# A decoder layer's weights: the low part made by an accumulating transfer instead of a subtraction

## The chip, the cores and the metric

The kernel runs on one core of a Trainium2 chip. The metric is the device time of one execution in microseconds; lower is better. An engine takes its instructions in the order in which the program gives them, and waits on semaphores for what other engines and transfers produce.

## The reference

One layer of a hybrid decoder on 512 tokens of width 1024, all in float32. The input is RMS-normalised and goes through one input projection. Three head groups read it: sparse attention (compressed, selected and window branches, with softmax and gates), a Mamba-2 SSD scan, and cross-attention to 256 memory tokens. Their outputs are gated, concatenated, projected back and added to the input, and normalised again.

```python
def reference(x, mem, positions, g_in, w_in, ...):
    xn = _rmsnorm(h, g_in[l])
    proj = xn @ w_in[l]
    (q_a, k_c, v_c, k_s, v_s, k_w, v_w, gate_logits, gate_a,
     z, xbc, dt, q_x, gate_x) = jnp.split(proj, split_at, axis=-1)
    o_a = _nsa_mixer(q_a, k_c, v_c, ...) * jax.nn.silu(gate_a)
    o_b = _ssd_mixer(z, xbc, dt, ...)
    o_c = _memory_attention(q_x, mem, ...) * jax.nn.silu(gate_x)
    h = h + jnp.concatenate([o_a, o_b, o_c], axis=-1) @ w_out[l]
    return _rmsnorm(h, g_final)
```

## The kernel before

**Two parts of each operand.** Matmuls run on operands of the type float32r, which holds fewer bits than float32. To keep the precision, every operand is split: `hi` is the value rounded to float32r, `lo` is the value minus `hi`. A product is then three matmuls: hi by hi, lo by hi, hi by lo.

**Weights come in chunks.** `chunk` (line 379) loads up to 1024 columns on 128 partitions (512 KB) into a staging tile `wst`, copies it to `whi` on ScalarE or VectorE (`X.copy`), and subtracts to get `wlo` on VectorE or GpSimd (`X.tensor_tensor`). There are 64 chunks. `wst` has two slots (`WS`), `whi` and `wlo` three each (`WH`). A slot is taken by the next chunk when the last reader of the old one is done: for `wst` that is the subtraction, for `whi` and `wlo` a matmul. The loads are issued by SP.

**Who uses them.** `proj_d` (line 450) takes one chunk for 128 output columns: eight steps of three matmuls on 512 columns, in the order hi, lo, hi, so that the lo part is needed in the second matmul. `z_half` takes three chunks at the start (the first half) and two later, and reads their lo parts last. `values` holds three chunks through its loop; `compress_mlp`, `mem_k` and `mem_v` are the short projections of the compressed and memory branches; `out_part` and `out_proj` make the output projection.

**Order.** Instructions are not issued where they are written. `Program` records them with their operands, and `issue` (line 173) places them by a list scheduler: each engine takes, of the instructions whose operands and slots are there, the first of the program (shifted by biases). `cost` (line 137) gives the scheduler a duration for each instruction and a time to land for each transfer; where two engines may run an instruction, the one that is free takes it, VectorE ahead of ScalarE and GpSimd. So a changed instruction or cost changes the whole order. All instructions are issued on one line, so the profile names nearly all of them L278, and tiles tell them apart. The stages, in time: the start and the first half of `z` to about 31 us; the SSD inputs and the second half of `z` to 92; compressed and memory keys and values beside the SSD scan to 182; keys and values of the other branches to 216; attention, woven with cross-attention and the output projection of two groups, to 440; the rest of the output projection.

Of the kernel before, what the change touches and what calls it, by code (L numbers as in the profile page):

```python
# [13 lines left out]
AF = mybir.ActivationFunctionType  # L14
OP = mybir.AluOpType
# [18 lines left out]
WMAX = 1024  # L34
# slots of the tags in SBUF and PSUM
B4, T2, M8, QB, PB, XB_, WS, WH = 2, 5, 12, 5, 4, 2, 2, 3
SB, TB, JB = 2, 2, 3
# shares at which streams are interleaved, and how far their instructions are put before (-) or
# behind (+) their place in the program when more than one could go
SA, SX, WA, WX, R1, R2 = 18.0, 55.0, 60.0, 128.0, 12.0, 5.0  # L40
# [34 lines left out]
class Program:  # L75
    """The instructions of a kernel, recorded in program order and issued in the order of a list
    scheduler: each engine takes, of the instructions whose operands and tiles are there, the
    first of the program. A tile takes a slot of its tag only if the tiles of the program before
    it still find theirs."""

# [31 lines left out]
    def record(self, *ways):  # L112
        """One instruction, with each engine that may run it: (engine, function, args, kw)."""
        eng, fn, args, kw = ways[0]
        outs = [a for a in (kw.get("out", args[0] if args else None), kw.get("accum_out")) if a is not None]
        ins = [a for a in list(args[0 if "out" in kw else 1:]) + [v for k, v in kw.items() if k not in ("out", "accum_out")]
               if hasattr(a, "tensor")]
        op = {"eng": eng, "fn": fn, "n": len(self.ops), "deps": set(), "bias": self.bias + BIAS.get((outs[0].tensor.name.rsplit("_", 1)[0], fn), 0), "tiles": set(),
              "args": args, "kw": kw, "ways": {w[0]: w + self.cost(w[0], w[1], outs, ins, w[3]) for w in ways}}
        op["cost"], op["tail"] = op["ways"][eng][4:]  # L120
        for aps, write in ((ins, False), (outs, True)):
            for a in aps:
                t, p0, p1, m = self.region(a)
                tl = self.tiles.setdefault(t, {"tag": None, "psum": False, "acc": [], "users": 0, "dram": True})
                op["tiles"].add(t)
                for o, w, q0, q1, m2 in tl["acc"]:
                    if (write or w) and o is not op and q0 < p1 and p0 < q1 and m & m2:
                        op["deps"].add(o["n"])
                tl["acc"].append((op, write, p0, p1, m))
        for t in op["tiles"]:  # L130
            tl = self.tiles[t]
            tl["users"] += 1
            if tl["users"] == 1 and tl["tag"] is not None:
                self.tags[tl["tag"]]["q"].append(t)
        self.ops.append(op)

    def cost(self, eng, fn, outs, ins, kw):
        n = 1
        for d in outs[0].shape[1:]:
            n *= d  # L140
        ps = any(self.tiles.get(a.tensor.name, {}).get("psum") for a in outs[:1] + ins)
        if fn == "dma_start":
            b = 4 * n * outs[0].shape[0]
            return 60.0, 2000.0 + b / 360.0
        if eng == "PE":
            if fn == "transpose":
                return 109.5, 158.0
            if ins[0].dtype == F32R:
                return max(109.5, 0.4167 * n + 2.5), 158.0
            return max(214.0 * ins[0].shape[1] / P, 1.667 * n), 158.0  # L150
        scalars = sum(1 for a in ins if hasattr(a, "tensor") and len(a.shape) == 2 and a.shape[1] == 1)
        if eng == "ACT":
            return (51.0 if ps else 93.0) + 0.833 * n + 93.0 * (scalars + ("accum_out" in kw)), 110.0
        if eng == "DVE":
            k = 1.04
            if fn == "reciprocal":
                k = 6.25
            elif fn == "tensor_reduce" or fn == "stream_shuffle":
                n = 1
                for d in ins[0].shape[1:]:  # L160
                    n *= d
            elif fn in ("tensor_copy", "tensor_scalar") and not ps:
                k = 0.52
            return 68.0 + k * n + 62.0 * scalars * (n > 1), 92.0
        if fn == "tensor_scalar" and scalars == 1:
            return 260.0 + 3.33 * n, 30.0
        if fn == "tensor_scalar":
            return 327.0 + 0.833 * n, 30.0
        if kw.get("op") == OP.pow:
            return 464.0, 30.0  # L170
        return 150.0 + 2.1 * n, 30.0
# [118 lines left out]
class AnyEngine:  # L290
    """Instructions that more than one engine can run."""

# [32 lines left out]
def hymba_kernel(ctx: ExitStack, tc: tile.TileContext, A, out):  # L325
# [3 lines left out]
    X = AnyEngine(prog)  # L329
# [7 lines left out]
    def f(ap):  # L337
        return ap.bitcast(F32)
# [8 lines left out]

# [1 line left out]
    def load_x(to, eng, i):  # L349
# [18 lines left out]

# [1 line left out]
    def biased(b, gen):  # L370
# [7 lines left out]

    def chunk(src, n, st=None, first=False):
        if st is None:  # L380
            st = wp.tile([P, WMAX], F32, name="wst", tag="wst", bufs=WS)[:, :n]
        SY.dma_start(st, src)
        hi = wp.tile([P, WMAX], F32R, name="whi", tag="whi", bufs=WH)[:, :n]
        lo = wp.tile([P, WMAX], F32R, name="wlo", tag="wlo", bufs=WH)[:, :n]
        if first:
            SC.activation(hi, st, AF.Copy)
        else:
            X.copy(hi, st)
        X.tensor_tensor(lo, st, f(hi), op=OP.subtract)
        return hi, lo  # L390

# [1 line left out]
    def rstd_of(ss, n, name):  # L393
# [26 lines left out]

# [1 line left out]
    rc = cp.tile([P, S], F32, name="rc")  # L422
# [23 lines left out]

# [1 line left out]
    done = set()  # L448
# [24 lines left out]

    # compressed keys and values: blocks of 32 tokens, every 16
    def compress_in(c0, pcol):
# [81 lines left out]

    # keys of the selected and the window branch
    def keys(b, c0):
# [13 lines left out]

    # values of both branches and the gates: token rows
    def values():
# [43 lines left out]

# [1 line left out]
    def cmp_soft(t):  # L621
# [40 lines left out]
    def soft(t, i, unit, den, ps2):  # L662
        """Scores of a unit of (head, branch) pairs and their exponentials, with the sums."""
        g, n, u = t // 2, i + 1, len(unit)
        s = pp.tile([P, u, n * P], F32, name="sc2", tag="s", bufs=SB)
        for x in range(0, u, 2):
            e, b = unit[x]
# [13 lines left out]
    def soft_div(t, i, units, den, ps):  # L681
        """Exponentials by their sums, times the gates."""
        gate = AT["gate"]
# [16 lines left out]
    def apply(t, i, ps2, pcs):  # L700
# [19 lines left out]
        if i % 2:  # L720
            # both parts together, times the gate path
            pov = O["po"]
# [45 lines left out]

# [1 line left out]
    def mem_turn(m):  # L770
# [101 lines left out]

# [1 line left out]
    SD = {}  # L874
# [87 lines left out]
    def z_half(hf):  # L962
# [6 lines left out]
        for c in range(3 - hf):  # L969
            n = min(kc_, KT - kc_ * c) * w_  # L970
            st = kp.tile([P, WMAX], F32, name="wst0", tag="m8", bufs=M8)[:, :n] if hf == 0 and c == 2 else None
            ch.append(chunk(A[f"wz{hf}"][c][:, :n], n, st, hf == c == 0))
            if hf == 0 and c < 2:
                load_x(xt, SY, 2 + c)
# [99 lines left out]

# [1 line left out]
    acc = []  # L1076

    def out_part(part):
        """The share of head group B or C, onto the residual."""
        if not acc:  # L1080
# [72 lines left out]
    def weave(a, b, ca, cb):  # L1153
        """Both streams, each at its share of the tensor engine's time."""
        pa = pb = 0.0
# [20 lines left out]
    def inter(a, b, ca, cb):  # L1176
        """Both streams as one, each at its share."""
        pa = pb = 0.0
# [63 lines left out]

# d-major columns of the input projection, by tiles of 128
DCOLS = [(c, P) for c in (KC, VC, KS, KW)]
# [5 lines left out]
def layout(inputs):  # L1250
    """The inputs as the program reads them: slices, transposes and packing only."""
    f32 = np.float32
# [3 lines left out]
    def rows(m, k, c):  # L1256
        # [k*128, c] -> [128, k*c]
        return m.reshape(k, P, c).transpose(1, 0, 2).reshape(P, k * c)
# [60 lines left out]
```

## Time and profile before

| | |
|---|---|
| time, median of 3 runs | 473.93 us (473.19 to 474.29) |
| profiled execution, first to last instruction | 473.4 us |
| TensorE / VectorE / ScalarE / GpSimd busy | 418.8 / 405.6 / 180.5 / 209.8 us |
| loaded from and written to HBM | 42.43 MB and 2.11 MB, 94 GB/s over the span |
| share of the 16 DMA engines' time, SP's queue | 28.6% |

The median of the runs is 0.5 us above the profiled span. Busy times of engines overlap. Matmuls are pipelined: a matmul's row is longer than the time until the next one starts.

### The profile page before, as it was taken

Reading aid. Unit: us, or ns where it says so; the run is one execution under the profiler, and the core shown is the slowest. Engines: PE = TensorE matmul, PEld = TensorE weight load, DVE = VectorE, ACT = ScalarE, POOL = GpSimd, SP = SyncE. Lnnn points to the kernel's source line nnn. Section 1 sums busy time; section 2 is a strip of 40 time slices with the busy share of each in tenths; the row PEclk is TensorE's granted clock in tenths of the full one; section 3 lists DMA queues with packets and bytes.
Section 4 is the critical chain, followed back from the end, with each engine's and each line's share of the span. In section 5 each row is a group of like instructions: output and inputs, shape, how many; then the busy total and the mean of one; then the engine's idle time right before and its main releaser. Section 6 shows DMA issues by size and latency. Waiting matters only on the chain.

```text
span 473.4 us, 6323 instructions
## 1 busy us (share of the span) xinstructions
PE 418.8 (88%) x2291; PEld 350.0 (74%) x2291; DVE 405.6 (86%) x701; ACT 180.5 (38%) x402; POOL 209.8 (44%) x137
## 2 busy tenths in 40 slices
PE   3798969898796999998998997989989999799993
PEld 3786869678785888896877775868678776687872
DVE  4897886998999998898789999897998999968555
ACT  5333232544224023444444344434444435322324
POOL 3671322367576675624443224233434626402332
PEclk9898979999999899999999999899999999999998
DMA  8714520333553444213120120132113202203104
GB/s 321 266 53 131 174 66 4 111 112 94 174 160 108 134 134 141 90 45 132 48 90 0 46 79 11 46 134 90 44 46 126 97 0 91 61 29 90 44 1 177
DMA packets 15407, 44.95 MB, mean 95 GB/s; under 512 B 1648, under 2 KB 3984, under 8 KB 15376
## 3 DMA queue, kind: packets, MB, share of 16 engines
q1 hardware_dynamic: 15232, 44.54, 28.6%
q8 instruction: 18, 0.29, 0.3%
q14 instruction: 13, 0.11, 0.1%
q10 hardware_dynamic: 144, 0.01, 0.0%
HBM read 42.43 MB, written 2.11 MB: 94 GB/s over the span
## 4 chain that ended last, share of the span: by engine, by line
PE 42%; DVE 40%; issue 5%; ACT 3%; POOL 2%; DMA 1%; POOLq 0%; DVEq 0%; ACTq 0%
PE pj L278 13%; PE po L278 9%; PE pop L278 5%; DVE wlo L278 5%; DVE whi L278 5%; PE pt L278 3%; DVE den L278 3%; DVE pr L278 3%; PE pjz L278 3%; PE sc L278 2%; PE pjv L278 2%; DVE cacc L278 2%; DVE nm L278 2%; DVE ptl L278 2%; DVE o L278 2%
## 5 line engine op out<-in xcount | busy, mean ns | idle before, releaser
L278 POOL TENSOR_TENSOR wlo<-wst,whi 128x1024 fp32r<-128x1024 f32 (+2 forms) x34 | 82.2, 2419 | 97.7 <-DVE whi L278 33.9
L278 PE MATMUL pj<-xh,whi 128*128 128x512 f32 x224 | 91.4, 408 | 0.0
L278 PE MATMUL pj<-xh,wlo 128*128 128x512 f32 x224 | 90.5, 404 | 0.4 <-DVE wlo L278 0.3
L278 PE MATMUL pj<-xl,whi 128*128 128x512 f32 x224 | 89.9, 401 | 0.0
L278 PEld LDWEIGHTS pj<-xh,wlo 128*128 128x128 f32 x224 | 42.7, 190 | 8.8 <-DVE wlo L278 0.9
L278 PEld LDWEIGHTS pj<-xl,whi 128*128 128x128 f32 x224 | 42.7, 191 | 8.6 <-issue 0.3
L278 PEld LDWEIGHTS pj<-xh,whi 128*128 128x128 f32 x224 | 42.7, 190 | 7.9 <-DVE gxt L278 0.4
L278 DVE TENSOR_TENSOR wlo<-wst,whi 128x1024 fp32r<-128x1024 f32 (+2 forms) x30 | 45.7, 1522 | 1.8 <-PE pjz L278 0.7
L278 ACT ACTIVATE pr<-sc,nm 128x128 f32<-128x128 f32 (+3 forms) x64 | 33.2, 525 | 36.1 <-DVE nm L278 16.5
L278 ACT ACTIVATE whi<-wst 128x1024 fp32r<-128x1024 f32 (+3 forms) x31 | 31.7, 1023 | 25.4 <-DMA wst<-in_wd 5.9
L278 PE MATMUL pt<-cst,pr 128*128 128x128 f32 x160 | 31.4, 279 | 8.7 <-DVE pr L278 6.9
L278 DVE CAST whi<-wst 128x1024 fp32r<-128x1024 f32 (+1 forms) x33 | 32.2, 977 | 6.6 <-PE pj L278 3.4
L278 PEld LDWEIGHTS pt<-cst,pr 128*128 128x128 f32 x160 | 19.4, 140 | 16.4 <-DVE pr L278 9.1
L278 PE MATMUL sc<-kst,qst 128*128 128x512 f32 (+2 forms) x96 | 29.5, 368 | 1.1 <-ACT pr L278 1.1
L278 DVE TENSOR_TENSOR ptl<-pt,pth 128x512 fp32r<-128x512 f32 x40 | 27.1, 682 | 1.4 <-ACT pth L278 1.0
L278 DVE TENSOR_REDUCE nm<-sc 128x1 f32<-128x384 f32 (+3 forms) x44 | 27.7, 633 | 0.3
L278 POOL TENSOR_SCALAR pr<-pr,den,gate 128x512 f32<-128x512 f32 (+1 forms) x11 | 9.0, 821 | 40.6 <-DVE den L278 24.9
L278 PE MATMUL pop<-whi,oph 128*128 128x512 f32 x64 | 26.4, 415 | 0.1
L278 ACT ACTIVATE pth<-pt 128x512 fp32r<-128x512 f32 x23 | 13.7, 596 | 33.2 <-PE pt L278 33.1
L278 PE MATMUL pop<-whi,opl 128*128 128x512 f32 x64 | 25.6, 403 | 0.0
L278 PE MATMUL pop<-wlo,oph 128*128 128x512 f32 x64 | 25.5, 401 | 0.0
L278 PE MATMUL po<-ptl,vst 128*128 128x256 f32 x80 | 22.0, 293 | 1.7 <-DVE ptl L278 1.7
(287 smaller groups left out, 1076.1 us busy)
## 6 DMA issues: line engine op xcount, KB each, us to landing
wst<-in_wd SPq DMA_DIRECT2D x28, 512.0 KB, 3.3
x<-in_x SPq DMA_DIRECT2D x8, 512.0 KB, 4.2
R<-a_rows SPq DMA_DIRECT2D x4, 512.0 KB, 4.3
wst<-in_w1k SPq DMA_DIRECT2D x4, 512.0 KB, 3.5
wst<-in_wmk SPq DMA_DIRECT2D x4, 512.0 KB, 3.6
wst<-in_w1v SPq DMA_DIRECT2D x4, 512.0 KB, 3.5
wst<-in_wmv SPq DMA_DIRECT2D x4, 512.0 KB, 3.6
wst<-in_wob SPq DMA_DIRECT2D x4, 512.0 KB, 3.6
```

Of the source, the lines that this page charges most:

```text
L278: o["ins"] = getattr(self.engines[o["eng"]].engine, o["fn"])(*o["args"], **o["kw"])
```

## The change

For all chunks but the first three (the first half of `z`), the subtraction goes. ScalarE writes the negated, rounded weights into `wlo` (`scale=-1.0`), the hi copy stays as it was, and GpSimd's queue issues a second transfer of the same weights from HBM that adds to what lies in `wlo`. The staging tile is now read by the two copies alone. The scheduler's costs get an entry for a transfer issued by GpSimd.

```diff
@@ cost
         if fn == "dma_start":
             b = 4 * n * outs[0].shape[0]
+            if eng == "POOL":
+                return 1000.0, 2000.0 + b / 180.0
             return 60.0, 2000.0 + b / 360.0
@@ chunk
-    def chunk(src, n, st=None, first=False):
+    def chunk(src, n, st=None, first=None):
...
         SY.dma_start(st, src)
         hi = wp.tile([P, WMAX], F32R, name="whi", tag="whi", bufs=WH)[:, :n]
         lo = wp.tile([P, WMAX], F32R, name="wlo", tag="wlo", bufs=WH)[:, :n]
-        if first:
-            SC.activation(hi, st, AF.Copy)
-        else:
-            X.copy(hi, st)
-        X.tensor_tensor(lo, st, f(hi), op=OP.subtract)
+        if first is not None:
+            if first:
+                SC.activation(hi, st, AF.Copy)
+            else:
+                X.copy(hi, st)
+            X.tensor_tensor(lo, st, f(hi), op=OP.subtract)
+            return hi, lo
+        SC.activation(lo, st, AF.Copy, scale=-1.0)
+        X.copy(hi, st)
+        G.dma_start(lo, src, accum_op=OP.add)
         return hi, lo
@@ z_half
-            ch.append(chunk(A[f"wz{hf}"][c][:, :n], n, st, hf == c == 0))
+            ch.append(chunk(A[f"wz{hf}"][c][:, :n], n, st, c == 0 if hf == 0 else None))
```

The rest of the diff takes out comments.

## Rows read from the trace of the kernel before

**Rows 1.** The page's busy time of each engine: us, share of the span, instructions.

```profile
PE 418.8 (88%) x2291; PEld 350.0 (74%) x2291; DVE 405.6 (86%) x701; ACT 180.5 (38%) x402; POOL 209.8 (44%) x137
```

**Rows 2.** The chain that ended last, whole span: shares by engine, then by line.

```profile
PE 42%; DVE 40%; issue 5%; ACT 3%; POOL 2%; DMA 1%; POOLq 0%; DVEq 0%; ACTq 0%
PE pj L278 13%; PE po L278 9%; PE pop L278 5%; DVE wlo L278 5%; DVE whi L278 5%; PE pt L278 3%; DVE den L278 3%; DVE pr L278 3%; PE pjz L278 3%; PE sc L278 2%; PE pjv L278 2%; DVE cacc L278 2%; DVE nm L278 2%; DVE ptl L278 2%; DVE o L278 2%
```

**Rows 3.** The same chain in two windows, 92 to 182 and 216 to 440 us.

```profile
by line: DVE wlo L278 20.6%; DVE whi L278 14.4%; PE pjm L278 8.0%; issue 7.4%; PE ph L278 5.6%; DVE cacc L278 4.6%; DMA wst<-in_wmk 4.0%; DMA wst<-in_wd 3.7%; DVE bct L278 2.6%; DVE kc L278 2.5%; PE pj L278 2.3%; DVE ft L278 2.3%; DVE vcs L
...
by line: PE pj L278 24.1%; PE pop L278 9.9%; PE po L278 8.0%; PE pt L278 6.3%; DVE den L278 5.7%; DVE pr L278 5.2%; PE sc L278 4.5%; DVE ptl L278 3.5%; DVE nm L278 3.4%; DVE o L278 3.2%; issue 3.2%; DVE xnm L278 2.3%; DVE whi L278 2.3%; DVE
```

**Rows 4.** Windows, all engines: stretch, length, busy (instructions) by engine, PEclk, DMA share, GB/s.

```profile
92.00:182.00 90.00, 76.86 (x502) 68.68 (x501) 83.57 (x106) 28.09 (x51) 59.15 (x36) 0.98 0.41 129
216.00:440.00 224.00, 210.08 (x1092) 167.25 (x1092) 200.18 (x394) 92.72 (x236) 83.58 (x54) 0.99 0.20 64
```

**Rows 5.** Windows for the instructions that touch `wlo`: PE, PEld, VectorE, GpSimd.

```profile
31.00:92.00 61.00, 26.88 (x88) 15.37 (x87) 5.04 (x5) 12.87 (x5) 0.92 0.32 100
92.00:182.00 90.00, 41.64 (x131) 25.45 (x131) 24.39 (x17) 12.34 (x5) 0.98 0.41 129
...
216.00:440.00 224.00, 70.51 (x174) 33.13 (x174) 4.41 (x3) 46.21 (x19) 0.99 0.20 64
```

**Rows 6.** Waits of SP's queue: us in total, times, longest.

```profile
SPq L278 <- POOL wlo L278: 222.9, 31, 15.3
```

**Rows 7.** The page's costliest groups: busy us, mean ns, idle before.

```profile
L278 POOL TENSOR_TENSOR wlo<-wst,whi 128x1024 fp32r<-128x1024 f32 (+2 forms) x34 | 82.2, 2419 | 97.7 <-DVE whi L278 33.9
...
L278 DVE TENSOR_TENSOR wlo<-wst,whi 128x1024 fp32r<-128x1024 f32 (+2 forms) x30 | 45.7, 1522 | 1.8 <-PE pjz L278 0.7
```

**Rows 8.** Instructions on tile `wst`: ns min/median/max, first and last start; landing of its loads.

```profile
L278 DVE CAST whi<-wst x33: 423/694/2506, 14.8 to 448.6; 128x1024 fp32r<-128x1024 f32 x32, 128x528 fp32r<-128x528 f32 x1
L278 ACT ACTIVATE whi<-wst x31: 672/1058/1073, 7.3 to 443.1; 128x1024 fp32r<-128x1024 f32 x26, 128x792 fp32r<-128x792 f32 x2, 128x840 fp32r<-128x840 f32 x2, 128x560 fp32r<-128x560 f32 x1
...
DMA to landing us min/median/max: 2.6/3.5/9.1
```

**Rows 9.** Instructions on tile `den`, 216 to 440 us: ns min/median/max.

```profile
L278 DVE TENSOR_SCALAR den<-den x26: 154/160/2166, 223.0 to 429.3; 128x2 f32<-128x2 f32 x23, 128x4 f32<-128x4 f32 x3
...
L278 DVE TENSOR_SCALAR pr<-pr,den,gate x21: 465/548/2502, 228.0 to 430.7; 128x384 f32<-128x384 f32 x11, 128x512 f32<-128x512 f32 x10
```

**Rows 10.** VectorE's groups by shape, 216 to 440 us: busy us, mean ns.

```profile
L278 DVE TENSOR_SCALAR den<-den 128x2 f32<-128x2 f32 x23 | 11.3, 492 | 0.9 <-ACT pr L278 0.8
L278 DVE CAST whi<-wst 128x1024 fp32r<-128x1024 f32 x10 | 8.7, 867 | 0.3 <-PE pj L278 0.2
L278 DVE TENSOR_SCALAR pr<-pr,den,gate 128x384 f32<-128x384 f32 x11 | 8.1, 761 | 0.1
L278 DVE TENSOR_SCALAR pr<-pr,den,gate 128x512 f32<-128x512 f32 x10 | 7.9, 806 | 0.1
```

**Rows 11.** A one-column instruction among GpSimd's groups, whole span.

```profile
L278 POOL TENSOR_TENSOR rx<-rx,mhalf 128x1 f32<-128x1 f32 x6 | 4.7, 781 | 7.3 <-DVE rx L278 6.5 <-DVE cwh L278 0.8
```

**Rows 12.** Windows, all engines, the first 20 us.

```profile
0.00:20.00 20.00, 10.30 (x51) 9.62 (x52) 12.17 (x25) 9.86 (x17) 11.52 (x13) 0.91 0.94 336
```

**Rows 13.** Timeline, 30 to 32 us: start, length, instruction.

```profile
30.61 1.23 DVE L278 TENSOR_TENSOR wlo<-wst,whi 128x1024 fp32r<-128x1024 f32 x1 [0.66 <-PE pjz L278]
...
31.89 0.50 PE L278 MATMUL pj<-xh,wlo 128*128 128x512 f32 x1 [0.25 <-DVE wlo L278]
```

**Rows 14.** Timeline, 207 to 217 us.

```profile
207.86 1.06 ACT L278 ACTIVATE whi<-wst 128x1024 fp32r<-128x1024 f32 x1 [0.99 <-PE pjv L278]
...
210.31 0.41 PE L278 MATMUL pj<-xh,wlo 128*128 128x512 f32 x1
```

**Rows 15.** Timeline, 448 to 456 us.

```profile
448.63 0.69 DVE L278 CAST whi<-wst 128x1024 fp32r<-128x1024 f32 x1
...
454.96 0.40 PE L278 MATMUL po<-wlo,oh 128*128 128x512 f32 x1
```

## The prediction, made before the changed kernel ran

> **What bounds the kernel now.** I read the busy times first [rows 1]: TensorE 88%, VectorE 86%, ScalarE 38%, GpSimd 44%. Two engines are near full, so the next view is the chain that ended last [rows 2]: 42% of it on TensorE and 40% on VectorE, with the weights' `wlo` and `whi` at 5.0% and 4.7% of 473.4 us, that is 24 and 22 us. What the change removes is therefore partly on the path. Where it is, the chain of two windows tells [rows 3]. From 92 to 182 us (compressed keys and values, memory keys and values, SSD) `wlo` is 20.6% and `whi` 14.4% of the window, 18.5 and 13.0 us, so four fifths of `wlo`'s share of the chain lie here. From 216 to 440 us (attention) `whi` has 2.3%, `wlo` is not among the parts listed, and `den` and `pr`, small VectorE work of the softmax, hold 10.9%.
>
> Then the stages. From 92 to 182 us VectorE is busy 83.6 of 90 us [rows 4], of which 24.4 are `wlo`, and 22 lo parts are made (17 on VectorE, 5 on GpSimd) [rows 5]: 4.1 us a chunk. The waits of SP's queue [rows 6] say how chunks follow one another: a load waits for a `wlo` (222.9 us in 31 waits for GpSimd's alone), because the subtraction is the last reader of the staging slot, and there are two slots.
>
> **What goes.** All subtractions but those of the first three chunks: 61 of 64. VectorE's 30 cost 45.7 us and GpSimd's 34 cost 82.2 [rows 7]; about 44 and 78 of these go. GpSimd's also cost VectorE: a `whi` cast takes 423 to 2506 ns with a median of 694 [rows 8], and the one-pass `den` instruction 154 to 2166 with a median of 160 [rows 9]; the long ones stand beside GpSimd work. In the attention stage I count 23 `den` x (492 - 160) = 7.6 us, 21 `pr` x (782 - 548) = 4.9 and 10 `whi` x (867 - 694) = 1.7 [rows 8 to 10], 14.2 us in all. The subtractions are 46.2 of GpSimd's 83.6 busy us there [rows 4, 5], 55%, so 7.8 us of this is theirs.
>
> **What comes.** Per chunk: a negating ScalarE copy, 1.06 us by the copy of the same shape [rows 8], so 61 x 1.06 = 64 us and ScalarE goes from 180.5 to about 244 us, 52%; it hides in ScalarE's idle time, and in the attention stage with it the exponentials queued behind. The `whi` copy stays; a busier ScalarE may leave more of them to VectorE (0 to 29 x 0.69 = 20 us; I take 4 us, since the negation is done first and VectorE is seldom free). And a transfer issued by GpSimd, in whose queue the softmax scalings and SSD products wait behind it. No GpSimd transfer is in this trace. Its issue I bound by nothing below and above by one of its subtractions, 2.4 us [rows 7]; I take 0.78, the mean of GpSimd's one-column instruction [rows 11], since an issue touches no data. The Trainium skill, "DMA: Bandwidth & Descriptors", section Specifications, gives about 1 us to the first byte on this path; with it each chunk below is 0.2 us later, which no run here shows.
>
> Its landing: a plain 512 KB load takes 3.5 us in the median, 2.6 at least and 9.1 at most [rows 8]. The accumulate also reads its destination. In the first 20 us the engines move 336 GB/s at a share of 0.94 [rows 12], so 512 KB occupy all sixteen for 524288 B / 357 GB/s = 1.47 us; a second read adds 0 to 1.47. I take it whole: 5.0 us. The Trainium skill, "Collectives: The Full Stack", section "The bandwidth ceiling", finds an adding transfer at about half of a copy's rate because of its two source reads; by that the sum is the same, and plain transfers alone, as here, cannot show it.
>
> So from a free `wlo` slot to a ready lo part: 1.06 + 0.78 + 5.0 = 6.8 us (2.6 + 1.06 = 3.7 to 9.1 + 1.06 + 2.4 = 12.6), against 1.2 to 2.4 for the subtraction. TensorE needs lo in the second matmul of a chunk, so this is a stall wherever a slot comes free just ahead of its use.
>
> **The places.**
> Start: the first new-style chunk's slot comes free at 30.61 and its lo part is first used at 31.89 [rows 13]. New: 30.61 + 6.8 = 37.4, +5.5 us (+2.4 to +11.3). Nothing covers it: TensorE has only this chunk.
> 31 to 92 us: VectorE loses 5.0 us of `wlo` [rows 5]; at the chain's 40% share, -2 (0 to -5).
> 92 to 182 us: four limits, each for 22 chunks. VectorE falls to 83.6 - 24.4 = 59 us and is out. Staging: a slot is free after load and copies, (3.5 + 1.06)/2 = 2.3 us a chunk, 50 us. The three `wlo` slots: (6.8 + about 1.5 of waiting in ScalarE's and GpSimd's queues + some 2 of use)/3 = 3.4 us, 76 us; the 1.5 is an estimate from GpSimd's 59 busy us of 90. The DMA engines: now 0.41 of the time [rows 4], 37 us; the accumulates add 22 x 1.47 to 22 x 2.94, so 69 to 102 us. With the second read whole it is 102, less about 10 for chunks whose transfers lie ahead of the window: 92, against 90 now. I take +2 (-21 to +12). So the work that VectorE loses here is replaced by transfers that take about as long.
> Behind the values' projection, whose three chunks hold all three slots: the next slot's copy starts at 207.9, lo is first used at 210.31 [rows 14]. New 214.7, +4.4; the scores and the softmax of attention's first tile are there to be put ahead, so I take +3 (0 to +8).
> Attention: VectorE loses 4.4 us of `wlo` [rows 5] and 7.8 of blocking, gets back 4 of `whi` and, if a transfer's issue blocks as GpSimd's other work does, 19 x 0.78 / 46.2 of the 7.8, 2.5. GpSimd, freed, takes scalings that either engine can run: of VectorE's 16 us of `pr` [rows 10] I take a quarter, 4. Together -9.7; of `den` and `pr`, whose rows make 27 us, the chain holds 24 (10.9% of 224), but a chain that is relieved in one place passes to TensorE, whose `pj` alone has 24.1% of it: I take two thirds, -6 (-16 to 0). The later lo parts are hidden here: a chunk comes every 11 us or so, three slots deep.
> End: the last chunk's copy starts at 448.63; 455.4 against a use at 454.96 [rows 15]: +0.5 (0 to +6).
> Sum: 5.5 - 2 + 2 + 3 - 6 + 0.5 = +3.0 on the profiled span of 473.4; the median of the runs, 473.93, is 0.5 us more, so 476.9, say 477.
>
> **Rivals.** *One: faster.* The accumulate costs the DMA engines what a plain load does (3.5 us to land, 1.47 of occupation). Then the dense window is 69 us, -21; the start +4, behind the values +1.5, the end 0; attention -13, 31 to 92 -4: 473.9 - 32 = 442 at the far end; with half of the window's gain and the -6 in attention it is 473.9 - 11 + 5.5 - 6 - 4 = 458. It decides if the landing is under about 4.5 us. For it: the chain, which has 31.5 us of `whi` and `wlo` in that window; against it: the destination has to be read too.
> *Two: slower by much.* The casts that last up to 2506 ns show that VectorE and GpSimd hold something from one another; if GpSimd's issue has to wait likewise for VectorE, which is busy 93% of the dense window, each lo part is up to 2.5 us later: 22 x 2.5/3 = 18 in the dense window, 2.5 at each of three turns: 477 + 26 = 503. The Trainium skill, "SBUF — State Buffer", section "SBUF: two separate sides", states just this of transfers issued by GpSimd: VectorE's two-port operations keep it from writing descriptors (0.62 us becomes 3.1). Against it: VectorE's casts of this kind are short, 0.69 us.
> *Three: no change.* Relief and delay cancel: 473.9.
> *Four: faster without the transfers' help.* The blocking counts for all of its length in attention, -16 in place of -6: 477 - 10 = 467. For it: `den` and `pr` are on the chain there. Against it: `pj` alone holds 24.1% of that chain.
> *Five: VectorE is not relieved,* since it takes nearly all `whi` copies (20 us back): attention and the early part give nothing, 477 + 8 = 485.
>
> **How the numbers follow.** The measurement tells 0.2%, 0.95 us, from no change. Forecast (slower, 475 to 489, its own range): 0.33. Rival one 0.26; two 0.12; three 0.08; four 0.15; five 0.06. Faster 0.26 + 0.15 = 0.41, same 0.08, slower 0.33 + 0.12 + 0.06 = 0.51. The two signs share the chance, so the range for 8 in 10 reaches into rivals one and two: 450 to 500, leaving out the far gain of rival one and the far end of rival two.
>
> **What would show it.** Of the changed profile: no `wlo` subtraction behind the third; 61 ScalarE `wlo` copies of 1.06 us; POOL's busy time down by some 78 us; `den` and `whi` means nearer their medians; issue to landing near 5 us (under 4.5 speaks for rival one, over 7.5 for two); a TensorE gap near 31 to 37 us on the first transfer; DMA share from 92 to 182 us at 0.9 or more; VectorE below 70% there. I am wrong if TensorE never waits for those transfers, or if the dense window shrinks by over 10 us.

## The result, and the profile of the changed kernel

The changed kernel takes 507.16 us (median of 4 runs, 504.22 to 516.37) against 474.11 (473.19 to 475.93) for the kernel before: a ratio of 1.0664 with a 95% interval of 1.0614 to 1.0715. Forecast were 477 us, with 450 to 500 as the range. The profiled execution is the longest of the four, so its stages lose 41 us where the medians differ by 33; in a run with the same edits up to the values' projection (e5_early below, span 504.5 us instead of 514.6) the stretch up to there is 6 us shorter.

The busy times and the chain that ended last, against [rows 1, 2], and the DMA queues (packets, MB, share of the 16 engines):

```profile
PE 433.7 (84%) x2291; PEld 364.0 (71%) x2291; DVE 352.7 (69%) x701; ACT 219.9 (43%) x436; POOL 167.9 (33%) x164
...
q0 software_dynamic: 8784, 31.56, 34.8%
q1 hardware_dynamic: 15232, 44.54, 26.8%
...
PE 51%; DMA 20%; DVE 12%; issue 8%; POOL 4%; ACT 4%; POOLq 0%; DVEq 0%; SPq 0%
PE pj L280 26%; DMA wlo<-in_wd 7%; PE pop L280 5%; PE po L280 4%; PE pt L280 3%; PE pjz L280 3%; PE sc L280 3%; DMA wlo<-in_wox 3%; DVE whi L280 2%; DMA wst<-in_wmv 2%; DMA R<-a_rows 2%; DMA wlo<-in_wmk 2%; DMA wlo<-in_w1v 2%; DVE o L280 1%; ACT wlo L280 1%
```

VectorE lost 53 us of work, and its share of the chain fell from 40% to 12%. In its place stand transfers, 20% of the chain where they had 1%. The accumulates' queue, q0, takes 34.8% of 514.6 us, 179 us for 61 chunks, 2.94 us each. A plain load of as many bytes takes 1.6: q1's 26.8% for 44.54 MB.

The windows of [rows 4], and the waits of TensorE (us in total, times, longest):

```profile
92.00:182.00 90.00, 67.06 (x359) 58.04 (x359) 58.19 (x83) 31.39 (x47) 41.65 (x39) 0.88 0.83 189
216.00:440.00 224.00, 209.53 (x1102) 171.02 (x1101) 179.65 (x394) 110.09 (x256) 62.24 (x64) 0.98 0.55 126
```

```profile
PE pj L280 <- DMA wlo<-in_wd: 19.0, 4, 9.6
```

In the dense window VectorE falls from 83.6 to 58.2 busy us and TensorE does 359 matmuls where it did 502: a resource was freed and less was done. The DMA engines' share doubles, to 0.83.

One new chunk, the first, in the timeline (start, length), against [rows 13]:

```profile
32.30 1.04 ACT L280 ACTIVATE wlo<-wst 128x1024 fp32r<-128x1024 f32 x1
...
33.66 1.05 POOL L280 DMA_DIRECT2D wlo<-in_wd  x1 [1.97 <-ACT th L280]
...
42.60 0.80 PE L280 MATMUL pj<-xh,wlo 128*128 128x512 f32 x1 [9.64 <-DMA wlo<-in_wd]
```

The negation takes 1.04 us, the issue follows 0.3 us behind it, and the lo part is there 8.9 us after the issue began; TensorE waits 9.64 us. Over all chunks, issue to landing, first of the transfers into `wlo`:

```profile
DMA to landing us min/median/max: 5.2/7.6/11.4
```

and of the loads into `wst`, which took 2.6/3.5/9.1 before [rows 8]:

```profile
DMA to landing us min/median/max: 2.6/5.5/9.8
```

Where the 41 us between the two spans lie, by the first matmul that reads the lo part of a kind of chunk (for `pjv` also the last matmul, for `pop` the first of any part). Times are in us; the runs are those of the next section, and those with four slots have eleven big tiles instead of twelve:

| stretch | before | after | small, 3 slots | 4 slots | 4 slots, plain | subtraction, 4 slots | late, 4 slots |
|---|---|---|---|---|---|---|---|
| start to the first `pj` with lo | 31.9 | 42.6 | 39.0 | 34.0 | 33.0 | 34.8 | 34.7 |
| to the values' projection (`pjv`) | 162.8 | 191.1 | 169.5 | 166.4 | 161.0 | 160.3 | 160.8 |
| the values' projection | 15.5 | 16.0 | 14.5 | 17.9 | 17.5 | 17.5 | 17.5 |
| its end to the first `pop` | 158.2 | 157.9 | 151.3 | 151.2 | 149.2 | 165.8 | 149.1 |
| to the end | 105.0 | 107.0 | 103.0 | 101.5 | 102.5 | 106.2 | 103.9 |
| span | 473.4 | 514.6 | 477.3 | 471.0 | 463.2 | 484.6 | 466.0 |

Of the 41.2 us, 10.7 are the start and 28.3 the stretch up to the values' projection.

### The profile page after: what moved, and what is told of

It reads as the page before. It is cut to its first block, busy times and chain, and to the rows that moved or that the text cites. A ratio compares the mean times of both kernels' runs of the same rounds, so it can differ in the third digit from the quotient of the medians.

```text
span 514.6 us, 6447 instructions
## 1 busy us (share of the span) xinstructions
PE 433.7 (84%) x2291; PEld 364.0 (71%) x2291; DVE 352.7 (69%) x701; ACT 219.9 (43%) x436; POOL 167.9 (33%) x164
## 3 DMA queue, kind: packets, MB, share of 16 engines
q0 software_dynamic: 8784, 31.56, 34.8%
q1 hardware_dynamic: 15232, 44.54, 26.8%
## 4 chain that ended last, share of the span: by engine, by line
PE 51%; DMA 20%; DVE 12%; issue 8%; POOL 4%; ACT 4%; POOLq 0%; DVEq 0%; SPq 0%
PE pj L280 26%; DMA wlo<-in_wd 7%; PE pop L280 5%; PE po L280 4%; PE pt L280 3%; PE pjz L280 3%; PE sc L280 3%; DMA wlo<-in_wox 3%; DVE whi L280 2%; DMA wst<-in_wmv 2%; DMA R<-a_rows 2%; DMA wlo<-in_wmk 2%; DMA wlo<-in_w1v 2%; DVE o L280 1%; ACT wlo L280 1%
## 5 line engine op out<-in xcount | busy, mean ns | idle before, releaser
L280 ACT ACTIVATE wlo<-wst 128x1024 fp32r<-128x1024 f32 (+2 forms) x61 | 63.8, 1046 | 112.5 <-PE pj L280 48.6
L280 PE MATMUL pj<-xh,wlo 128*128 128x512 f32 x224 | 93.4, 417 | 19.0 <-DMA wlo<-in_wd 19.0
L280 PE MATMUL pj<-xh,whi 128*128 128x512 f32 x224 | 93.2, 417 | 3.4 <-DVE whi L280 3.1
L280 PE MATMUL pj<-xl,whi 128*128 128x512 f32 x224 | 91.5, 408 | 0.0
L280 DVE CAST whi<-wst 128x1024 fp32r<-128x1024 f32 (+1 forms) x41 | 36.9, 901 | 34.6 <-PE pj L280 22.7
L280 POOL DMA_DIRECT2D wlo<-in_wd x28 | 25.0, 892 | 104.1 <-ACT wlo L280 94.3
L280 DVE CAST pth<-pt 128x512 fp32r<-128x512 f32 x23 | 15.8, 688 | 20.8 <-PE pt L280 20.6
L280 POOL TENSOR_SCALAR pr<-pr,den,gate 128x512 f32<-128x512 f32 (+1 forms) x14 | 11.3, 807 | 45.8 <-DVE den L280 39.5
L280 PE MATMUL po<-pth,vst 128*128 128x256 f32 x80 | 22.7, 288 | 3.7 <-DVE pth L280 3.7
L280 ACT ACTIVATE whi<-wst 128x1024 fp32r<-128x1024 f32 (+3 forms) x23 | 22.9, 1000 | 3.3 <-PE pjz L280 3.3
```

The costliest lines, as they stand in the source:

```text
L280: o["ins"] = getattr(self.engines[o["eng"]].engine, o["fn"])(*o["args"], **o["kw"])
```

## Experiments

The kernel before was timed again beside these runs, with medians of 474.75 to 475.73 us; ratios are against those.

### What one transfer costs

**e1_probe.** No layer is computed; single transfers of 512 KB run one at a time, and then in company.

```diff
+nc.gpsimd.dma_start(x, A[r], accum_op=OP.add)      # alone, three times
+nc.gpsimd.dma_start(x, A[3], accum_op=OP.add)      # two in flight
+nc.gpsimd.dma_start(y, A[4], accum_op=OP.add)
+nc.gpsimd.dma_start(x, A[5], accum_op=OP.add)      # beside two loads of SP
+nc.sync.dma_start(l1, A[6])
+nc.sync.dma_start(l2, A[7])
```

> This kernel does nothing of the layer: it only loads 512 KB weight tiles, one transfer at a time and then in company. It asks what an accumulating transfer costs by itself. Theory L (latency: the 7.6 us in the changed kernel are what such a transfer takes even alone, and three lo slots cannot cover it): the accumulate takes 6.5 to 8 us alone from issue to landing, the half-sized one over 5.5, and company adds under 1 us. Theory O (occupation: the engines have too many bytes to move): about 5 us alone (3.5 for a load, 1.5 for the second read), half-sized about 4; 7.5 or more beside another accumulate or beside two loads of SP, and those loads go from 3.5 to 5 or more. Theory S (VectorE's casts hold up GpSimd's issue): about 5 us alone and 7.5 or more beside ten casts, with an issue that lengthens from 0.9 us. GpSimd's plain transfer: L 5 us or more, O and S about 4.

The page's DMA issues (count, KB each, median us from issue to landing):

```profile
sp<-in_wd SPq DMA_DIRECT2D x3, 512.0 KB, 3.2
plain<-in_wd POOLq DMA_DIRECT2D x3, 512.0 KB, 3.6
acc<-in_wd POOLq DMA_DIRECT2D x3, 512.0 KB, 5.1
mixl<-in_wd SPq DMA_DIRECT2D x2, 512.0 KB, 4.4
castacc<-in_wd POOLq DMA_DIRECT2D x2, 512.0 KB, 5.5
half<-in_wd POOLq DMA_DIRECT2D x3, 256.0 KB, 3.6
...
pairy<-in_wd POOLq DMA_DIRECT2D x1, 512.0 KB, 5.1
pairx<-in_wd POOLq DMA_DIRECT2D x1, 512.0 KB, 7.1
mixacc<-in_wd POOLq DMA_DIRECT2D x1, 512.0 KB, 8.1
```

Alone an accumulate lands 5.1 us after its issue began, 1.5 later than the plain copy of the same queue. Half the bytes take 1.5 us less. Beside two loads it takes 8.1, and the loads 4.4 instead of 3.2. Beside ten casts of VectorE, issued with it, it takes 5.5. So company on the DMA engines is enough to explain the 7.6 us in the kernel. Ten casts of VectorE, the mechanism of rival two, account for 0.4.

### Which part of the transfer the kernel pays for, with three slots

**e2_plain** and **e3_small** keep the changed kernel's order and replace the accumulate, one by a plain transfer of as many bytes, the other by an accumulate of 64 columns.

```diff
@@ issue, ahead of each instruction
+if o["eng"] == "POOL" and o["fn"] == "dma_start":
+    o["kw"] = {}                                        # e2_plain
+    o["args"] = tuple(v[:, :64] for v in o["args"])     # e3_small
```

> The changed kernel with each accumulate replaced by a plain transfer of the same bytes from GpSimd's queue, in the same order of instructions; the lo part is then the whole weight and not the remainder. Theory O: the occupation halves, landing falls to about 4.5 us and the time to 475 to 485. Theory L, if the latency is that of GpSimd's path and not of the adding: landing stays over 6 us and the time stays over 497. Theory S: as L, landing over 6 us in the window where VectorE casts.

> The changed kernel, same order of instructions, with each accumulate cut to the first 64 of up to 1024 columns, so one sixteenth of the bytes; the rest of the lo part stays the negated weight. The first lo matmul of a chunk still waits for its transfer. Theory O: landing about 3 us, time 460 to 475, since nearly all added occupation is gone. Theory L: landing over 5.5 us, time 490 or more. Theory S: landing over 5 us where VectorE casts, time 490 or more.

The plain transfer gives 486.32 us, a ratio of 1.0224 (1.0155 to 1.0293), and lands in 4.7 us; the small one 479.87, 1.0104 (1.005 to 1.0157), and lands in 3.4. Both are slower than theory O had put down, and well below theories L and S. So of the 32 us above the 475.02 of before, 21 go with the second read, 6 with the other bytes, and 5 stay even when hardly a byte is moved. The small one has the attention stage at 151.3 us, 6.9 less than before. VectorE's relief is there: the one-pass `den` instruction takes at most 0.17 us in that stage, where it took up to 2.17 [rows 9]. With the full accumulate it takes no more, but the stage is 157.9 us long.

**e6_smallplan.** The small accumulate, with the scheduler told its cost.

```diff
@@ cost, for a transfer of GpSimd's queue, in e3_small
-                return 1000.0, 2000.0 + b / 180.0
+                return 880.0, 3400.0
@@ issue: 3300 of it fixed, 100 on the engines
```

> As the run with an accumulate of 64 columns only (the output is without most of the lo part), but the scheduler is told the small transfer's cost too (0.88 us to issue, 3.4 us to land, no bytes) where before it went on planning 2.9 us of DMA time for each. That run still lost 16 us between the first matmul of head group B's side and the values' projection, though the bytes were gone. Theory order (the planned order, made for a dear transfer, is what still costs): the stage comes back to about the kernel before's and the relief of VectorE shows, 465 to 473 us. Theory slots (three slots, each held from the negation over the issue to the landing, some 7 us that no order removes): no change, 477 to 483 us.

478.84 us, 1.009 (1.0059 to 1.0122). An order planned for the small transfer does not bring the last 5 us back.

### Where in the kernel

**e4_late** makes the lo parts by the transfer in the attention stage alone (23 chunks), **e5_early** up to the values' projection alone (34 chunks, not the 38 of its text).

```diff
@@ chunk
-        if first is not None:
+        if first is not None or not mode[0]:
...
@@ e4_late (e5_early: True to begin with, False ahead of this weave)
+    mode[0] = True
     weave(biased(BA, attention()), xa(), WA, WX)
+    mode[0] = False
```

> The accumulating transfer only for the chunks of the attention stage (keys done to the output projection of two groups, 23 chunks), the subtraction everywhere else. By both theories the late lo parts are hidden in attention, where the two kernels took the same time from the first values matmul to the end of that stage (247.9 and 247.5 us), including a wait of 9 us for the first accumulate. So 468 to 475 us. If the accumulate costs something in attention too that its relief of VectorE pays for, the same time comes out with DMA waits in the chain; if the loss came from a general slowdown of the engines, over 485.

> The accumulating transfer is used for every chunk up to the values' projection, 38 of the 61 that the change moves, and the subtraction by an engine again in the attention stage and behind it; with the run that has it only in the attention stage this splits the change in two. Theory A (the loss is made where loads already fill the DMA engines, up to the values' projection, and nothing is lost or won behind it): the two halves add up, so all of the 32 us are here, 503 to 510 us. Theory B (half of the loss is the later stages', hidden in the other run because there the dense stage ran as before): 488 to 497 us. Theory C (the attention stage gains only if the stage ahead of it is not late): below 485 us.

Late: 474.16 us, 0.9977 (0.9945 to 1.0009), no difference that can be told. Early: 506.67, 1.0697 (1.0651 to 1.0742), the whole loss. The two add up to the whole (the last four chunks are in neither), so the loss has been made by the end of the values' projection.

### The order, or the slots

**e7_cost** tells the scheduler what the trace shows of the accumulate.

```diff
@@ cost, for a transfer of GpSimd's queue; issue: 4700 of it fixed
-                return 1000.0, 2000.0 + b / 180.0
+                return 880.0, 4700.0 + b / 180.0
```

> The changed kernel with the scheduler told what the trace shows: 0.88 us to issue and 4.7 us of fixed time behind 2.9 us of transfer, instead of 1.0 and 2.0. Theory occupation (the DMA engines are full from 92 to 250 us, so no order helps): 502 to 511 us, and the share of the DMA engines there stays above 0.8. Theory order (the order is made for a transfer that lands 2.7 us earlier, and matmuls wait for it): 490 to 500 us, and the matmuls' waits for the transfer of the projections' weights go from some 39 us to under 20.

504.19 us, 1.0598 (1.0526 to 1.067): the interval overlaps that of the changed kernel. Theory order's second sign did come: TensorE's waits for the transfers from `in_wd`, matmuls and weight loads together, fell from 39.1 to 10.1 us. Yet only some 3 us came back. A better informed order moves the waits and is no way out.

**e8_wh4** gives hi and lo a fourth slot; **e10_m11** makes the room for it alone.

```diff
-B4, T2, M8, QB, PB, XB_, WS, WH = 2, 5, 12, 5, 4, 2, 2, 3
+B4, T2, M8, QB, PB, XB_, WS, WH = 2, 5, 11, 5, 4, 2, 2, 4    # e8_wh4
+B4, T2, M8, QB, PB, XB_, WS, WH = 2, 5, 11, 5, 4, 2, 2, 3    # e10_m11
```

> The changed kernel with four slots for hi and lo instead of three; the room comes from the big tiles' tag, which goes from 12 to 11 slots. Theory slots (a chunk's time from free slot to ready lo, about 10 us, over three slots is what TensorE waits for): a third more in flight, waits for the weights' transfers at least halved, 485 to 496 us. Theory occupation (4.4 us of all DMA engines for each chunk, 39 chunks in 150 us and other traffic on top): one more in flight only makes each land later, as two at once did alone (5.1 and 7.1 us); 502 to 512 us, the landing's median 8 us or more.

> The changed kernel with eleven slots for the big tiles, and three for hi and lo as before: the other half of what the run with four slots changed. Theory slots: nothing comes back, 502 to 511 us. Theory tiles (it was the other order that eleven big tiles force, not the slots): 472 to 490 us.

Four slots: 473.16 us, 0.9971 (0.9946 to 0.9996). Eleven big tiles alone: 517.5, 1.0787 (1.0708 to 1.0867). The fourth slot is worth 44 us, more than the whole loss. The direction is that of theory slots, but both results lie outside its ranges: the slot gave back more, and the missing big tile cost 10 us that no theory had. (`WH` gives the hi part a fourth slot too; no run gave it to the lo part alone, or a third slot to the staging tile.) The accumulates land no sooner; on tile `wlo` of the run with four slots:

```profile
DMA to landing us min/median/max: 4.9/7.5/10.5
```

Its dense window:

```profile
92.00:182.00 90.00, 74.59 (x457) 67.12 (x455) 54.72 (x91) 33.47 (x55) 50.36 (x46) 0.87 0.94 214
```

The accumulates took the DMA engines 38.0% of its span of 471.0 us, again 2.93 us a chunk, and the engines were simply busier, 0.94 instead of 0.83. So with three slots they had not been the limit. What had been is seen at ScalarE's negations, each the first to write a slot: what ended ScalarE's idle time before them (us, times), from 92 us to the end of the values' projection, first with three slots, then with four:

```profile
  PE pjm L280: 17.0, 5
  PE pj L280: 15.8, 7
  PE ph L280: 13.2, 3
  DMA wst<-in_w1k: 10.0, 2
  DMA wst<-in_wmv: 9.0, 2
```

```profile
  PE ph L280: 6.6, 2
  DMA wst<-in_wd: 4.5, 3
  DMA wst<-in_w1v: 3.8, 1
  PE pjv L280: 3.0, 2
```

With three, 46 us end with a matmul that lets go of a slot (or, for part of `pj`, of other work), and 19 with a late load; with four, 12.5 and 10.8 in all.

**e9_before_wh4** and **e13_before_m11** are the same two edits on the kernel before.

> The kernel before, with its subtractions, with four slots for hi and lo and eleven for the big tiles, as the run of the changed kernel that came back to 473 us. Theory slots (three slots were too few only because a chunk takes 9 us from a free slot to a ready lo with the accumulating transfer; the subtraction takes 2 to 4, so three suffice): 471 to 477 us, no gain. Theory room (a fourth slot helps any form of the kernel, so the change still costs what it costs): 455 to 467 us.

> The kernel before with eleven slots for the big tiles and three for hi and lo: the corner that is missing of two kernels by two and two (the changed kernel took 507 us, with eleven tiles 517, with eleven and a fourth slot 473; the kernel before 475, with eleven and a fourth slot 487). Theory slots (the fourth slot is worth 44 us to the accumulating transfer and nothing to the subtraction, and eleven tiles cost either kernel some 10 us): 483 to 491 us. Theory room (the fourth slot helps the subtraction as well): 495 us or more. Theory order (with the subtraction the fourth slot itself costs, by the other order that it makes): 472 to 480 us.

e9_before_wh4 took 486.92 us, 1.0238 (1.0198 to 1.0278), above the ranges of both its theories; e13_before_m11 took 487.78, 1.0259 (1.0211 to 1.0308), as theory slots has it. The medians side by side:

| | 12 big tiles, 3 slots | 11 big tiles, 3 slots | 11 big tiles, 4 slots |
|---|---|---|---|
| subtraction | 475 | 487.8 | 486.9 |
| accumulate | 507.2 | 517.5 | 473.2 |

The fourth slot gives the accumulate 44 us and the subtraction 0.9, less than their ranges tell apart. The big tile that pays for it costs 10 to 13. With four slots and like tiles the change gains 13.7 us; against the kernel before, with its twelve tiles, it gains some 2.

### What is left with four slots

**e14_plain_wh4** and **e15_small_wh4** are e2_plain and e3_small with e8_wh4's slots; **e11_cost_wh4** is e7_cost with them.

> With four slots and eleven big tiles, the accumulate replaced by a plain transfer of as many bytes into lo (lo then holds the weights themselves, so the output is another); with three slots that took 486 us against 507. Theory hold (the second read costs only by the time that it holds a slot, so with four slots it costs nothing): 469 to 477 us, the same as the accumulate's 473. Theory bytes (1.5 us more of all DMA engines for each of 38 chunks still lies on the path in the stage whose DMA share is 0.94): 450 to 465 us.

> With four slots and eleven big tiles, the accumulate cut to 64 columns (the output is without most of the lo part); with three slots that took 480 us. Theory hold: 466 to 477 us, at most 7 us under the full accumulate's 473. Theory bytes: 435 to 460 us.

> The changed kernel with four slots, and the scheduler told the measured 0.88 us of issue and 4.7 us of fixed time. Theory occupation last (with four slots the stretch from 92 to 182 us already has its DMA engines 94% busy, so an order that knows the landing finds nothing more there): 470 to 477 us. Theory order (with three slots the true costs gave 3 us; here too): 465 to 470 us.

Plain: 463.8 us, 0.9765 (0.9728 to 0.9801). Small: 465.67, 0.9805 (0.9764 to 0.9845). Neither theory has it whole: the plain transfer lies in the range of theory bytes, the small one at the edge of theory hold's. The second read still costs 9.4 us, 473.2 against 463.8, where it cost 21; the other bytes cost nothing, where they cost 6. These three kernels issue in the same order. The plain one's dense window, with the DMA engines at 0.69:

```profile
92.00:182.00 90.00, 75.69 (x472) 68.89 (x471) 56.66 (x91) 35.10 (x57) 45.72 (x46) 0.89 0.69 228
```

The measured costs in the scheduler made it slower than either theory had, 484.88 us, 1.0173 (1.0123 to 1.0222): an order alone can move this kernel by 12 us, so a few us between variants with orders of their own say little.

**e12_late_wh4** is e4_late with e8_wh4's slots.

> Four slots, and the accumulating transfer only from the attention stage on, 23 chunks, the subtraction by an engine elsewhere. Theory both (the second reads go where the DMA engines are half idle, the early stage keeps its subtractions, and the fourth slot lets VectorE's relief in attention show): 462 to 470 us. Theory relief lost (the attention stage is TensorE's, with little of VectorE's time on the chain that the subtraction holds up): 471 to 477 us.

467.54 us, 0.9828 (0.9791 to 0.9865): 1.7% under the kernel before. The accumulate stands where the DMA engines are half idle (a share of 0.49 from 216 to 440 us), and the attention stage takes 149.1 us, against 165.8 for the subtraction with the same slots and tiles. How much of this is the relief and how much another order, no run separates.

## Why the prediction was wrong

**The step that failed** is "92 to 182 us", and in it the limit of the three `wlo` slots: "(6.8 + about 1.5 of waiting in ScalarE's and GpSimd's queues + some 2 of use)/3 = 3.4 us, 76 us". It was put under that of the DMA engines, 92 us, which came out level with the 90 of before. Slots go round, so a slot's cycle can be read from the traces: from the first write of a lo part until it is ready, and from then until the chunk three (or four) later is written. Means over the 15th to the 37th chunk, all 23 between the SSD inputs and the keys and values of the other branches:

| | until ready, us | until the next write, us | slots | cycle over slots | from chunk to chunk, us |
|---|---|---|---|---|---|
| before | 1.8 | 12.1 | 3 | 4.6 | 4.79 |
| after | 9.3 | 8.5 | 3 | 5.9 | 6.02 |
| small | 5.3 | 10.6 | 3 | 5.3 | 5.38 |
| four slots | 9.6 | 11.6 | 4 | 5.3 | 5.04 |
| four slots, plain | 7.1 | 13.0 | 4 | 5.0 | 4.78 |

The last two columns agree by arithmetic, whatever the limit is. Whether the slots are the limit shows in the second column, split by the matmuls that read each lo part. The split is for the 20 of these chunks ahead of the values' projection, each kind's matmuls counted off in order; "at once" is within 0.5 us:

| | until ready, us | waits to be read | is read | slot lies free | read at once | written again at once |
|---|---|---|---|---|---|---|
| before | 1.9 | 2.4 | 3.2 | 5.3 | 11 of 20 | 0 of 20 |
| after | 9.6 | 2.5 | 3.6 | 1.4 | 9 of 20 | 12 of 20 |
| small | 5.3 | 5.6 | 3.3 | 0.8 | 0 of 20 | 15 of 20 |
| four slots | 9.6 | 3.4 | 3.5 | 3.8 | 6 of 20 | 4 of 20 |
| four slots, plain | 7.1 | 5.3 | 3.5 | 3.4 | 0 of 20 | 5 of 20 |

Before, a slot lay free for 5.3 us of its cycle. After, 12 of 20 slots are written again as soon as they are let go, and 9 of 20 lo parts are read as soon as they are ready: much of the time both ends wait for the ring. With four slots they lie free again. In the small one the slots are refilled at once too, but its lo parts wait 5.6 us for TensorE, so the slots alone do not explain its last 5 us.

The term that was mis-sized is the use. A lo part holds its slot for 6.1 us after it is ready (2.5 until its first matmul and 3.6 of reading), not "some 2", and the trace of before had 5.6 of this: the term was guessed where it could have been read. With 5.6 the prediction's own 8.3 us until ready would have given 13.9/3 = 4.6 us a chunk, 102 us for 22 chunks, and the slots as the first limit, ahead of the 92 us of the DMA engines; the sum would have been some 487 us, slower but still short of the 507. The second error is 1 us in the time until ready: issue and landing were put at 0.78 + 5.0 = 5.8 us, and take 5.1 for a transfer alone, but 7.6 in the kernel beside its loads, whose landing goes from 3.5 to 5.5; part of this was covered by the 1.5 us of queueing. 23 x (6.02 - 4.79) = 28.3 us, so the whole loss of the stretch up to the values' projection lies in these chunks. In e5_early, at 5.82 us a chunk, that stretch loses 22.5.

**What was sized right.** The accumulate's occupation: 2.94 us of all sixteen engines a chunk forecast, 2.94 measured. That it fits so closely is luck: the plain transfer takes 1.61 us (e2_plain, 20.4% of 480.5 us for 61 chunks), not 1.47, and the second read adds 1.33. The Trainium skill, "Collectives: The Full Stack", section "The bandwidth ceiling", has an adding transfer at about half of a copy's rate. The traces come near it, at 1.61/2.94 = 0.55. The issue: 0.88 us against 0.78. VectorE's fall, so rival five is out. The attention stage's relief: -6 forecast, -6.9 with the small accumulate. With four slots it is -14.6 against the subtraction with like slots and tiles (151.2 against 165.8), more than twice the forecast, and here the orders differ too.

**What was not.** The start: +5.5 forecast, +10.7 measured, in the first chunk's issue and landing (8.9 us for 5.8) and in a negation that starts 1.7 us later than the slot was put free (32.30 for 30.61); the bound of +11.3 held it. Behind the values' projection the same, +3 forecast:

```profile
247.27 2.24 ACT L280 ACTIVATE wlo<-wst 128x1024 fp32r<-128x1024 f32 x2 [0.85 <-PE pjv L280]
...
248.63 0.90 POOL L280 DMA_DIRECT2D wlo<-in_wd  x1 [2.84 <-ACT wlo L280]
...
257.82 0.79 PE L280 MATMUL pj<-xh,wlo 128*128 128x512 f32 x1 [4.40 <-DMA wlo<-in_wd]
```

The lo part is read 8.1 us behind the last `pjv` matmul; it was 0.1 before, 4.1 with the small accumulate and 0.4 with four slots. Of the 6.6 us by which the attention stage is longer than with the small accumulate, 4.0 are this wait; for the rest no cause is shown. From 31 to 92 us -2 was forecast; the stretch from the first `pj` to the first `pjm` with lo went from 78.9 to 80.9.

**The rivals.** One (the accumulate as cheap as a plain load) is out by 2.94 us of occupation; even a plain load lost 11 us with three slots. Two forecast 503 us, near what came, by a mechanism that the probe puts at 0.4 us for a transfer; that it came near is luck. The Trainium skill, "SBUF — State Buffer", section "SBUF: two separate sides", has a transfer issued by GpSimd grow from 0.62 to 3.1 us beside a VectorE copy. The probe does not bear this out for these casts: the issue grew from 0.86 to 1.17 us and the landing from 5.1 to 5.5. Three and four are out. The signs that I gave were half right: GpSimd's busy time fell by 42 us, not 78 (its own 61 issues of 0.88 us, which the page of the profile counts as busy, had been left out); issue to landing above 7.5 us was to speak for rival two, and spoke for company on the DMA engines; a share of 0.9 or more from 92 to 182 us was to show the DMA engines as the limit, and 0.83 was measured until a fourth slot made it 0.94.

**What stays open.** Why the second read still costs 9.4 us with four slots: the DMA share of 0.94 in that window suggests that there the engines are the limit after all, but no run took other traffic away from them. Below the plain transfer's share of 0.69, fewer bytes gave nothing more. And why the twelfth big tile is worth 10 to 13 us.

## What to carry to other kernels

When a step behind a ring of slots is swapped for one with a longer latency, work out the cycle first: time until ready plus time in use, over the number of slots, against the time from one chunk to the next. Read the use from the trace, from the moment a part is ready to its last read; the time until the next write also holds time in which the slot lies free. With two streams interleaved, a part waits for its turn and its matmuls are drawn apart: here the use was 6 us where 2 had been guessed. A transfer's latency is to be read beside the traffic that it will meet, and a change that frees an engine may need one more slot before the freed time shows. Here the same change gains 14 us with four slots and loses 33 with three, each against the subtraction with like slots and tiles.

## What the runs showed of the hardware beyond that

TensorE lost time behind its waits too. After the 9.64 us wait that ends at 42.60 us its granted clock is at half, 1.2 GHz, for 5 us, and `pj` matmuls start 0.43 us apart; from 48.6 us it is at 2.4 GHz and they start 0.23 apart. The two stretches in the windows view (TensorE's clock is the third number from the end):

```profile
42.60:47.80 5.20, 5.20 (x12) 4.14 (x13) 0.00 (x0) 0.00 (x0) 0.00 (x0) 0.50 1.00 247
48.60:58.80 10.20, 10.20 (x51) 8.40 (x50) 4.94 (x11) 5.09 (x10) 1.72 (x2) 1.00 0.49 109
```

Over the span the mean clock is 0.932 (0.975 before), and TensorE's busy time grows from 418.8 [rows 1] to 433.7 us with the same 2291 matmuls: up to 15 of the 41 us are a slower TensorE behind its stalls, on top of the stalls. With four slots it is 419.6.

Two accumulates in flight come one behind the other: in the probe the one issued at 66.80 us landed after 5.1, as alone, the one at 67.34 after 7.1, 2.5 us later, near the 2.94 us that one keeps the engines. And an accumulate costs GpSimd more to issue than a plain transfer, 0.86 us against 0.55, and 1.17 beside VectorE's casts. The second of the two in flight took 1.20 with VectorE idle, so VectorE is not the only thing that makes an issue longer.
